# One transformer block on one core: gate and up weights in quarters, two of their sums made by adding transfers, one block more by seven products

## The chip, the core and the metric

The kernel runs on one core of a Trainium2 chip. A core has a matrix engine (TensorE, in the profile PE, with weight loads as PEld), a vector engine (VectorE, DVE), a scalar engine (ScalarE, ACT), GpSimd (POOL) and SyncE (SP). SP and POOL here issue the transfers between the chip's main memory and SBUF, the memory on the core; TensorE writes its products to banks of PSUM, which VectorE and ScalarE read. Each engine works through a fixed list of instructions in order and waits at semaphores. The metric is the device time of one execution in microseconds.

## What is computed

One layer of a hybrid encoder block on 512 tokens of width 1024: a token mixer with two kinds of attention, cross-attention into 256 memory tokens, and a gated FFN with an inner width of 2816. Each has a norm before and after it, and its result is added to the stream. All inputs and outputs are float32. What the change touches is the FFN's first half:

```python
D_MODEL = 1024
D_FF = -(-8 * D_MODEL // 768) * 256          # 2816

def swiglu(h, w_gate_up, w_down):
    g, u = jnp.split(h @ w_gate_up, 2, axis=-1)
    return (jax.nn.silu(g) * u) @ w_down

    h = rms_norm(x, g_ffn_pre[l])
    x = x + rms_norm(swiglu(h, w_gate_up[l], w_down[l]), g_ffn_post[l])
```

## The kernel before

**Numbers in two pieces.** Every float32 factor is split into a rounded piece (`hi`, made by a ScalarE cast to fp32r) and the rest (`lo`, a VectorE subtraction). A product is then three matmuls, hi by hi, hi by lo and lo by hi (`mm3`, lines 139 to 142). Activations are split once and stay in SBUF. Weights are loaded in float32, split, and used.

**The FFN's first half.** The 5632 columns of gate and up weights are worked in 22 blocks of 256 columns, gate and up in turn: block n has columns `(n % 2) * FF + (n // 2) * 256` on. A block is a product of 1024 x 256 weights with the normalised activations, 1024 x 512. Cut into two by two quarters on both sides (four k-blocks of 128 rows by 128 columns for the weights, four k-blocks by 256 tokens for the activations `b11`, `b21`, `b12`, `b22`), it is eight products of 4 x 3 matmuls each (`eight`), 96 matmuls of 128 rows by 256 columns. In `seven` the same result comes from seven such products, 84 matmuls, by Winograd's form of Strassen's method: some products take sums of weight quarters (s1 to s4) and sums of activation quarters (t1 to t4, made once), and VectorE adds the products up. Blocks 0 and 1 are loaded and worked ahead (`load_unit`, `first_ffn`); 2, 3 and 11 are done by `eight`, the other 17 by `seven`.

**Weights on their way.** For a block by seven, `seven_weights` makes four items for a ring in SBUF (`ring_hi`, `ring_lo`): the quarter a11; the sums s2 and s4; the upper row of quarters; and the sums s3 and s1. `load_raw` brings the block by two SP transfers of 512 KB, `lower` and `upper`, in three rotating raw buffers (tag `raw`), with runs of 256 floats in main memory. VectorE makes the four sums (lines 929 to 932) into one of the two halves of the tile `sums`, chosen by the block's parity. Each item is then split into the ring by a ScalarE cast and a VectorE subtraction (lines 902 and 903). A ring slot is filled again once the products that read it are done; single slots for a11 number two, double slots three. `take` emits the fills in the program as slots become free; the framework then puts each engine's instructions in order by priority and inserts the semaphores.

**Products and banks.** `seven` (line 1116) uses four banks. The first product goes to p17's left half, the second to p26's right half, the third to p35's left half, the fourth to p26's left half; then VectorE reads all of p26 (line 1128) and the left half of p35 (line 1129). Products five and six follow, with lines 1134 and 1135 reading them. The seventh goes to p35's right half (line 1137) and is read at line 1138. A product that writes a bank waits until its earlier content has been read. Gate blocks use banks with tags a and o and end in a Silu on ScalarE, up blocks use s and t and end in two multiplications (lines 1148 and 1150).

The tile `sums` takes the place of `y`, the cross-attention's output, in SBUF (tag `sB`). After the 22 blocks comes the product with `w_down`, whose weights use the same ring. POOL has no work in the stretch of the blocks.

Of the kernel before, what the change touches and what calls it, by code (L numbers as in the profile page):

```python
# [36 lines left out]
def hybrid_block_kernel(  # L37
# [33 lines left out]
    def f32(ap):  # L71
        return ap.bitcast(F32)
# [23 lines left out]
    def later(n):  # L96
        tc.cur_priority += n
        try:
            yield
        finally:  # L100
            tc.cur_priority -= n

    units = []
    loaded = []

    def load_unit(w, k0, nkb, c0, ncol, dst=None, skip=0):
        u = len(loaded)
        if dst is None:
            def place(name):
                flat = wp.tile([P, KB * 256 + 48], F32R, tag=name, name=f"{name}{u}", bufs=2)  # L110
                return flat[:, skip : skip + nkb * ncol].rearrange("p (k n) -> p k n", k=nkb)

            hi, lo = place("hi"), place("lo")
        else:
            hi, lo = dst()
        step = nkb if nkb * ncol <= 1024 else 4 if ncol < 512 else 2
        j = 0
        for n in [min(step, nkb - k) for k in range(0, nkb, step)]:
            raw = wp.tile([P, n, ncol], F32, tag="raw", name=f"raw{u}_{j}", bufs=3)
            r0 = (k0 + j) * P  # L120
            nc.sync.dma_start(
                raw,
                w[r0 : r0 + n * P, c0 : c0 + ncol].rearrange("(k p) n -> p k n", p=P),
            )
            act.copy(hi[:, j : j + n, :], raw)  # L125
            dve.tensor_tensor(out=lo[:, j : j + n, :], in0=raw, in1=f32(hi[:, j : j + n, :]), op=ALU.subtract)  # L126
            j += n
        loaded.append((hi, lo))
# [98 lines left out]
    with tc.tile_pool(name="mix", bufs=1, reuse_waits="tile") as bp:  # L227
# [75 lines left out]
        raws = {0: load_v(0, 1)}  # L303
# [77 lines left out]
        for b in range(3):  # L381
            l = bp.tile([P, 2, SEQ], F32R, tag=f"L{b}", name=f"L{b}")
# [206 lines left out]
        order = [(0, g) for g in fox_order] + [(1, 0), (1, 1)]  # L589
        for n, (side, g) in enumerate(order):  # L590
            with later(-20):
                q, kt, kl, v = group_proj(f"{side}{g}")
            if n == 3:
# [4 lines left out]
                for k in range(0, KB, 2):  # L598
                    b = msq[:, 2 * (k > 0) : 2 * (k > 0) + 2, :]
# [44 lines left out]
    with tc.tile_pool(name="cross", bufs=1, reuse_waits="tile") as cp:  # L644
# [249 lines left out]
        def item(at, size, fill):  # L894
            items.append((at, at + size, fill))

        def fill_from(at, shape, src, order=None):
            def fill():
                h, l = split(at, None, shape)
                h2, l2 = (a.rearrange(order) for a in (h, l)) if order else (h, l)  # L900
                v = src()
                act.copy(h2, v)  # L902
                dve.tensor_tensor(out=l2, in0=v, in1=f32(h2), op=ALU.subtract)  # L903
                return h, l

            return fill
# [7 lines left out]
        def double():  # L914
            nslot[1] += 1
            return AS_WEIGHTS + 1024 + 1024 * (nslot[1] % 3)

        def seven_weights(n, c0):
            raw, total = {}, sums[:, n % 2]
            s2, s4, s3, s1 = (total[:, i] for i in range(4))  # L920

            def a11():
                raw["lower"] = load_raw(w_gate_up, 0, 4, c0, 256)
                raw["upper"] = load_raw(w_gate_up, 4, 4, c0, 256)
                return raw["lower"][:, :, :P]

            def s2_s4():
                lower, upper = raw["lower"], raw["upper"]
                dve.tensor_tensor(out=s1, in0=lower[:, :, P:], in1=upper[:, :, P:], op=ALU.add)
                dve.tensor_tensor(out=s2, in0=s1, in1=lower[:, :, :P], op=ALU.add)  # L930
                dve.tensor_tensor(out=s4, in0=s2, in1=upper[:, :, :P], op=ALU.add)
                dve.tensor_tensor(out=s3, in0=lower[:, :, :P], in1=lower[:, :, P:], op=ALU.add)
# [5 lines left out]
            item(at := double(), 1024, fill_from(at, two, lambda: raw["upper"], "p c k n -> p k c n"))  # L938
            item(at := double(), 1024, fill_from(at, two, lambda: total[:, 2:4]))

        def eight_weights(n, c0):
            for k0 in (0, 4):
                item(
                    at := double(), 1024,
                    fill_from(at, dict(k=4, n=256), lambda k0=k0: load_raw(w_gate_up, k0, 4, c0, 256)),
                )

        EIGHT = (2, 3, 11)
        for n in range(2, FB):
            (eight_weights if n in EIGHT else seven_weights)(n, (n % 2) * FF + (n // 2) * 256)  # L950

# [100 lines left out]
        for pair in range(2):  # L1052
            ns = slice(pair * 256, (pair + 1) * 256)
            for b in range(2):
                cs = slice(b * P, (b + 1) * P)
                for acc, (wh_, wl_) in zip(accs[b], first_ffn):
                    for k in range(KB):
                        mm3(
                            acc[:, ns], wh_[:, k, cs], wl_[:, k, cs],
                            bt[pair][:, k // 4, 0, k % 4, :], bt[pair][:, k // 4, 1, k % 4, :], k == 0, k == KB - 1,  # L1060
                        )
# [17 lines left out]
        def eight(tags, done):  # L1079
            accs = [bank(tag) for tag in tags]  # L1080
            for half, bs in enumerate(((b11, b12), (b21, b22))):
                ((h, l),) = take()
                for m in range(2):
                    w = [a[:, :, m * P : (m + 1) * P] for a in (h, l)]
# [28 lines left out]
        def twice(a):  # L1113
            return bass.AP(a.tensor, a.offset, [list(a.ap[0]), [0, 2], list(a.ap[-1])])

        def seven(O, tags, done):

            p17, p26, p35, p4 = (bank(tag) for tag in tags)
            v = cp.tile([P, 256], F32, tag="v", name="v", bufs=2)
            (a11,) = take()  # L1120
            product(p17[:, left], a11, b11)
            act.copy(v, p17[:, left])
            ((h, l),) = take()
            product(p26[:, right], (h[:, 0], l[:, 0]), t2)
# [3 lines left out]
            dve.tensor_tensor(out=O[:, 0], in0=halves(p26), in1=twice(v), op=ALU.add)  # L1128
            dve.tensor_tensor(out=O[:, 1, 0], in0=p35[:, left], in1=O[:, 0, 1], op=ALU.add)
# [8 lines left out]
            dve.tensor_tensor(out=O[:, 1], in0=twice(p35[:, right]), in1=O[:, 1], op=ALU.add)  # L1138
            done(1, 0)
            done(1, 1)  # L1140

# [225 lines left out]
```

## Time and profile before

| | |
|---|---|
| runs | 789.24, 1262.61, 787.30 us; median 789.24 |
| the profiled execution, its own time | 786.43 us |
| its span in the profile | 784.0 us |
| granted TensorE clock, mean | 0.998 of full speed |
| read from main memory | 77.13 MB |
| stretch of the blocks by seven, first to last | 482.57 to 660.52 us |

The run of 1262.61 us is disturbed and is not used. The span runs from the program's first instruction to its last; the execution's own time, 786.43 us, has 2.4 us around it.

How to read it: an engine's busy time counts its instructions from start to end, with overlaps counted once. A matmul's row begins when it starts to stream and ends when its last result is out, so rows of matmuls that follow closely overlap, and the pace of TensorE is read from the distance of starts. A group's row gives line, engine, operation, the tile written and the tiles read, shapes, how often, busy time, mean ns of one, and the idle time just before with what ended it. Transfers are shown with the line and queue that issued them and the time from issue to landing.

### The profile page before, as it was taken

The numbers are of one execution on the slowest core, as the hardware profiler recorded it, in microseconds if no ns is written. First come the engines' busy times: TensorE is split into PE (matmuls) and PEld (weight loads), VectorE is DVE, ScalarE is ACT, GpSimd is POOL, SyncE is SP. The second block draws the span as 40 slices with busy tenths as digits, with TensorE's granted clock in tenths as the row PEclk, the third lists the DMA queues.
The fourth block names the chain that finished last, engine by engine and source line by source line (L and its number), as shares of the span: only waits on it lengthen the run. The fifth ranks groups of instructions, "written<-read, shape, count | busy, mean of one in ns | idle before, by whom it ended". The sixth has DMA issues, their size and how long they took to land.

```text
span 784.0 us, 12758 instructions
## 1 busy us (share of the span) xinstructions
PE 762.2 (97%) x4958; PEld 678.8 (87%) x4958; DVE 592.9 (76%) x1073; ACT 425.4 (54%) x774; POOL 71.1 (9%) x110
## 2 busy tenths in 40 slices
PE   8999999999999999999999999999999999999996
PEld 8887788888778888877778899999999999898985
DVE  6567889879887588545663779998899989986626
ACT  7358888757875348444553635554444446543411
POOL 6001231110321101000001100000000000000001
PEclk9999999999999999999999999999999999999999
DMA  7341112412322725421350202332433332241302
GB/s 245 82 133 55 54 55 68 136 67 80 109 68 92 275 105 164 132 77 58 109 174 14 81 28 82 107 109 81 135 109 108 108 110 105 84 161 55 137 25 108
DMA packets 60747, 80.04 MB, mean 102 GB/s; under 512 B 2704, under 2 KB 43664, under 8 KB 60688
## 3 DMA queue, kind: packets, MB, share of 16 engines
q1 hardware_dynamic: 59264, 74.49, 29.2%
q0 software_dynamic: 1280, 4.72, 1.7%
q8 instruction: 39, 0.64, 0.3%
q14 instruction: 20, 0.16, 0.1%
q10 hardware_dynamic: 144, 0.02, 0.0%
HBM read 77.13 MB, written 2.10 MB: 101 GB/s over the span
## 4 chain that ended last, share of the span: by engine, by line
PE 72%; DVE 11%; ACT 7%; issue 4%; DMA 3%; POOL 2%; SPq 0%; DVEq 0%; POOLq 0%; ACTq 0%
PE ps_a L141 14%; PE ps_a L140 14%; PE ps_a L142 14%; PE ps_s L142 4%; PE ps_s L140 4%; PE ps_s L141 4%; DVE ring_lo L903 3%; PE ps_t L534 2%; PE ps_t L140 2%; PE ps_t L141 2%; PE ps_t L142 2%; DMA raw<-in_dram 2%; PE ps_o L543 2%; PE ps_s L515 1%; PE ps_o L140 1%
## 5 line engine op out<-in xcount | busy, mean ns | idle before, releaser
L902 ACT CAST ring_hi<-fraw 128x1024 fp32r<-128x1024 f32 (+1 forms) x62 | 57.5, 932 | 64.3 <-PE ps_t L142 17.6
L126 DVE TENSOR_TENSOR lo<-raw,hi 128x1024 fp32r<-128x1024 f32 x56 | 68.2, 1224 | 22.3 <-ACT hi L125 22.0
L903 DVE TENSOR_TENSOR ring_lo<-fraw,ring_hi 128x1024 fp32r<-128x1024 f32 (+1 forms) x62 | 66.5, 1076 | 21.4 <-ACT ring_hi L902 21.0
L142 PE MATMUL ps_a<-hTh,lo 128*128 128x512 f32 x192 | 76.8, 400 | 0.6 <-DVE lo L126 0.6
L141 PE MATMUL ps_a<-hTl,hi 128*128 128x512 f32 x192 | 76.1, 396 | 0.0
L140 PE MATMUL ps_a<-hTh,hi 128*128 128x512 f32 x192 | 75.9, 395 | 0.1
L125 ACT CAST hi<-raw 128x1024 fp32r<-128x1024 f32 x56 | 57.8, 1048 | 23.9 <-PE ps_a L141 15.0
L902 ACT CAST ring_hi<-sums 128x1024 fp32r<-128x1024 f32 x34 | 35.7, 1050 | 54.9 <-PE ps_a L141 24.2
L903 DVE TENSOR_TENSOR ring_lo<-sums,ring_hi 128x1024 fp32r<-128x1024 f32 x34 | 41.6, 1223 | 4.3 <-ACT ring_hi L902 4.1
L142 PEld LDWEIGHTS ps_a<-hTh,lo 128*128 128x128 f32 x192 | 36.1, 188 | 7.3 <-DVE lo L126 1.0
L141 PEld LDWEIGHTS ps_a<-hTl,hi 128*128 128x128 f32 x192 | 36.1, 188 | 6.3
L140 PEld LDWEIGHTS ps_a<-hTh,hi 128*128 128x128 f32 x192 | 36.2, 188 | 6.1 <-ACT hi L125 0.3
L529 ACT ACTIVATE p<-p,nm 128x128 f32<-128x128 f32 (+1 forms) x64 | 36.2, 565 | 8.4 <-DVE nm L519 7.6
L140 PE MATMUL ps_a<-b,ring_hi 128*128 128x256 f32 x140 | 38.8, 277 | 0.0
L141 PE MATMUL ps_a<-b,ring_hi 128*128 128x256 f32 x140 | 38.8, 277 | 0.0
L142 PE MATMUL ps_a<-b,ring_lo 128*128 128x256 f32 x140 | 38.8, 277 | 0.0
L140 PE MATMUL ps_s<-b,ring_hi 128*128 128x256 f32 x128 | 35.5, 277 | 0.0
L141 PE MATMUL ps_s<-b,ring_hi 128*128 128x256 f32 x128 | 35.5, 277 | 0.0
L142 PE MATMUL ps_s<-b,ring_lo 128*128 128x256 f32 x128 | 35.5, 277 | 0.0
L536 ACT CAST pth<-ps_t 128x128 fp32r<-128x128 f32 (+1 forms) x64 | 27.0, 424 | 14.5 <-PE ps_t L534 13.8
L537 DVE TENSOR_TENSOR ptl<-ps_t,pth 128x128 fp32r<-128x128 f32 (+1 forms) x64 | 30.7, 487 | 5.0 <-ACT pth L536 3.7
L534 PE MATMUL ps_t<-ident,p 128*128 128x128 f32 x160 | 28.1, 275 | 1.1 <-DVE p L531 0.8
(534 smaller groups left out, 2619.8 us busy)
## 6 DMA issues: line engine op xcount, KB each, us to landing
raw<-in_dram SPq DMA_DIRECT2D x64, 512.0 KB, 3.6
fraw<-in_dram SPq DMA_DIRECT2D x62, 512.0 KB, 3.5
cb<-in_dram SPq DMA_DIRECT2D x8, 256.0 KB, 2.6
xo<-in_dram POOLq DMA_DIRECT2D x4, 512.0 KB, 5.5
out_dram<-yd SPq DMA_DIRECT2D x8, 256.0 KB, 2.0
rawv<-in_dram SPq DMA_DIRECT2D x3, 520.0 KB, 6.2
xt<-in_dram SPq DMA_DIRECT2D x3, 512.0 KB, 6.9
gb<-in_dram POOLq DMA_DIRECT2D x3, 512.0 KB, 4.8
```

The costliest lines, as they stand in the source:

```text
L125: act.copy(hi[:, j : j + n, :], raw)
L126: dve.tensor_tensor(out=lo[:, j : j + n, :], in0=raw, in1=f32(hi[:, j : j + n, :]), op=ALU.subtract)
L140: pe.matmul(dst, sh, mh, start=first, stop=False)
L141: pe.matmul(dst, sh, ml, start=False, stop=False)
L142: pe.matmul(dst, sl, mh, start=False, stop=last)
L529: act.activation(p[:, :n], p[:, :n], AF.Exp, bias=nm, scale=-1.0, accum_out=sm)
L534: pe.transpose(tp[:, k * P : (k + 1) * P], p[:, k * P : (k + 1) * P], ident)
L536: act.copy(span(ph, i), t3)
L537: dve.tensor_tensor(out=span(pl, i), in0=t3, in1=f32(span(ph, i)), op=ALU.subtract)
L543: pe.matmul(acc[:, a:], v[:, k, vh, :], m[:, k * PTS + a : k * PTS + SEQ], start=k == 0 and m is ph, stop=k == NT - 1 and m is pl,)
L902: act.copy(h2, v)
L903: dve.tensor_tensor(out=l2, in0=v, in1=f32(h2), op=ALU.subtract)
```

## The change

On the host, `w_gate_up` is laid out anew before the launch, so that each quarter of a block (128 partitions by 4 x 128 floats) lies in contiguous rows of 2 KB. Quarter (r, m) of the block is k-blocks 4r to 4r + 3 and columns 128m to 128m + 127. All reads of gate and up weights go through the new function `quarters`.

In `seven_weights` the four sums become two: s2 and s4 stay on VectorE. s1 and s3 are made by transfers: SP loads quarter (0, 1) into each, then POOL issues a transfer that adds quarter (1, 1) to s1 and quarter (0, 0) to s3. a11 has a load of its own (256 KB), and the lower k-blocks' other half is read twice, once for each sum; the row of quarters with r = 1 is one load of 512 KB (`raw["upper"]`). Items are split in the order in which they are loaded, without the reordering of before.

Block 11 is done by `seven` instead of `eight`. In `seven`, the last product goes to p26's left half instead of p35's right half. The functions that work by eight products read their weights in the new order.

```diff
+    def quarters(c, r, m=None):
+        row = (c // 256 * 2 + r) * 2 * P
+        if m is None:
+            return w_gate_up[row : row + 2 * P, :].rearrange("(m p) n -> p m n", p=P)
+        return w_gate_up[row + m * P : row + (m + 1) * P, :]
...
+            if w is w_gate_up:
+                nc.sync.dma_start(raw.rearrange("p k n -> p (k n)").rearrange("p (m n) -> p m n", m=2), quarters(c0, j // 4))
+            else:
+                nc.sync.dma_start(
...
+        def load_half(c0, r):
+            raws[0] += 1
+            raw = wp.tile([P, 2, 4 * P], F32, tag="raw", name=f"fraw{raws[0]}", bufs=3)
+            nc.sync.dma_start(raw, quarters(c0, r))
+            return raw.rearrange("p c (k n) -> p c k n", k=4)
...
             def a11():
-                raw["lower"] = load_raw(w_gate_up, 0, 4, c0, 256)
-                raw["upper"] = load_raw(w_gate_up, 4, 4, c0, 256)
-                return raw["lower"][:, :, :P]
+                raws[0] += 1
+                raw["a11"] = wp.tile([P, 4, P], F32, tag="raw", name=f"fraw{raws[0]}", bufs=3)
+                nc.sync.dma_start(flat(raw["a11"]), quarters(c0, 0, 0))
+                for s, (r, m) in ((s1, (1, 1)), (s3, (0, 0))):
+                    nc.sync.dma_start(flat(s), quarters(c0, 0, 1))
+                    nc.gpsimd.dma_start(flat(s), quarters(c0, r, m), accum_op=ALU.add)
+                raw["upper"] = load_half(c0, 1)
+                return raw["a11"]
 
             def s2_s4():
-                lower, upper = raw["lower"], raw["upper"]
-                dve.tensor_tensor(out=s1, in0=lower[:, :, P:], in1=upper[:, :, P:], op=ALU.add)
-                dve.tensor_tensor(out=s2, in0=s1, in1=lower[:, :, :P], op=ALU.add)
-                dve.tensor_tensor(out=s4, in0=s2, in1=upper[:, :, :P], op=ALU.add)
-                dve.tensor_tensor(out=s3, in0=lower[:, :, :P], in1=lower[:, :, P:], op=ALU.add)
+                dve.tensor_tensor(out=s2, in0=s1, in1=raw["a11"], op=ALU.add)
+                dve.tensor_tensor(out=s4, in0=s2, in1=raw["upper"][:, 0], op=ALU.add)
                 return total[:, 0:2]
...
-        EIGHT = (2, 3, 11)
+        EIGHT = (2, 3)
...
-            product(p35[:, right], (h[:, 1], l[:, 1]), t1)
-            dve.tensor_tensor(out=O[:, 1], in0=twice(p35[:, right]), in1=O[:, 1], op=ALU.add)
+            product(p26[:, left], (h[:, 1], l[:, 1]), t1)
+            dve.tensor_tensor(out=O[:, 1], in0=twice(p26[:, left]), in1=O[:, 1], op=ALU.add)
...
+    at = len(arrs) - len(_WEIGHTS) + _WEIGHTS.index("w_gate_up")
+    arrs[at] = arrs[at].reshape(2, 4, P, -1, 2, P).transpose(3, 0, 4, 2, 1, 5).reshape(-1, 4 * P)
```

More of the change, by code (lines that the diff above doesn't have):

```diff
@@ L120, in load_unit @@
             r0 = (k0 + j) * P
[L121 to L124, printed above, removed]
+            if w is w_gate_up:
+                nc.sync.dma_start(raw.rearrange("p k n -> p (k n)").rearrange("p (m n) -> p m n", m=2), quarters(c0, j // 4))
+            else:
+                nc.sync.dma_start(
+                    raw,
+                    w[r0 : r0 + n * P, c0 : c0 + ncol].rearrange("(k p) n -> p k n", p=P),
+                )
             act.copy(hi[:, j : j + n, :], raw)
@@ L895, in item, with fill_from @@
             items.append((at, at + size, fill))
-        def fill_from(at, shape, src, order=None):
+        def fill_from(at, shape, src):
             def fill():
                 h, l = split(at, None, shape)
-                h2, l2 = (a.rearrange(order) for a in (h, l)) if order else (h, l)
                 v = src()
-                act.copy(h2, v)
-                dve.tensor_tensor(out=l2, in0=v, in1=f32(h2), op=ALU.subtract)
+                act.copy(h, v)
+                dve.tensor_tensor(out=l, in0=v, in1=f32(h), op=ALU.subtract)
                 return h, l
@@ L916, in double, with flat @@
             return AS_WEIGHTS + 1024 + 1024 * (nslot[1] % 3)
+        def flat(a):
+            return a.rearrange("p k n -> p (k n)")
+        def load_half(c0, r):
[3 more added lines that the diff above has]
+            return raw.rearrange("p c (k n) -> p c k n", k=4)
         def seven_weights(n, c0):
@@ L937, in seven_weights @@
             item(at := double(), 1024, fill_from(at, two, s2_s4))
-            item(at := double(), 1024, fill_from(at, two, lambda: raw["upper"], "p c k n -> p k c n"))
+            item(at := double(), 1024, fill_from(at, two, lambda: raw["upper"]))
             item(at := double(), 1024, fill_from(at, two, lambda: total[:, 2:4]))
         def eight_weights(n, c0):
[L942 to L946, printed above, removed]
-        EIGHT = (2, 3, 11)
+            for r in range(2):
+                item(at := double(), 1024, fill_from(at, dict(c=2, k=4, n=P), lambda r=r: load_half(c0, r)))
+        EIGHT = (2, 3)
         for n in range(2, FB):
@@ L1083, in eight @@
                 for m in range(2):
-                    w = [a[:, :, m * P : (m + 1) * P] for a in (h, l)]
+                    w = [a[:, m] for a in (h, l)]
                     for n, ns in enumerate((left, right)):
```

9 lines of the change are left out of this document (6 added, 3 removed).

## The prediction

> **What bounds the kernel now.** I read the page first, then a table of time windows over the stage that the change touches, then single instructions of TensorE (PE) and VectorE (DVE) in it. The page gives the span and each engine's load.
>
> ```profile
> span 784.0 us, 12758 instructions
> PE 762.2 (97%) x4958; PEld 678.8 (87%) x4958; DVE 592.9 (76%) x1073; ACT 425.4 (54%) x774; POOL 71.1 (9%) x110
> PE 72%; DVE 11%; ACT 7%; issue 4%; DMA 3%; POOL 2%; SPq 0%; DVEq 0%; POOLq 0%; ACTq 0%
> ```
>
> TensorE is busy for 97% of the span and is 72% of the chain that ended last, so the time is TensorE's work plus its waits. The change touches the gate and up products of the FFN. In the windows below, the first row holds the whole run of blocks from the first one done by seven products to the last; the others are single blocks. The columns are stretch, its length, and for each engine busy time (instructions), then the granted clock, DMA share and GB/s. Instructions that overlap a border are counted on both sides, so counts run two or three high.
>
> ```profile
> 482.57:660.52 177.95, 176.19 (x1526) 174.69 (x1525) 165.23 (x238) 87.29 (x132) 0.00 (x0) 1.00 0.33 104
> 482.57:492.77 10.20, 9.80 (x86) 9.61 (x85) 9.63 (x14) 5.20 (x7) 0.00 (x0) 1.00 0.32 103
> 551.92:562.80 10.88, 10.88 (x99) 10.88 (x97) 9.28 (x14) 3.77 (x6) 0.00 (x0) 1.00 0.49 150
> 562.80:572.32 9.52, 9.52 (x87) 9.52 (x85) 8.77 (x12) 4.36 (x6) 0.00 (x0) 1.00 0.35 109
> 611.92:621.70 9.78, 9.78 (x86) 9.78 (x85) 9.30 (x14) 4.87 (x8) 0.00 (x0) 1.00 0.34 109
> ```
>
> 551.92:562.80 is block 11, the one block of this stretch still done by eight products; 562.80:572.32 is block 12, by seven, with no wait in it. The stretch holds 17 blocks of seven and one of eight. Free of waits they would take 17 x 9.52 + 10.88 = 172.72 us; they took 177.95. So 5.23 us are lost here. One loss looks like this (start, length, engine, line, matmul, and the idle time before it with what ended it):
>
> ```profile
> 490.50 0.28 PE L141 MATMUL ps_a<-tlo,ring_hi 128*128 128x256 f32 x1
> 490.62 0.28 PE L142 MATMUL ps_a<-tlo,ring_lo 128*128 128x256 f32 x1
> 491.29 0.39 PE L140 MATMUL ps_a<-thi,ring_hi 128*128 128x256 f32 x1 [0.40 <-DVE G L1129]
> ```
>
> Starts go from 0.12 us apart to 0.67: the seventh product, which writes the right half of bank p35, waits until VectorE has read that bank's left half (line 1129). VectorE was late because a sum of weights stood between:
>
> ```profile
> 489.62 0.69 DVE L1128 TENSOR_TENSOR G<-ps_a,v 128x512 f32<-128x512 f32 x1
> 490.22 0.68 DVE L931 TENSOR_TENSOR sums<-sums,fraw 128x512 f32<-128x512 f32 x1
> 490.82 0.42 DVE L1129 TENSOR_TENSOR G<-ps_a,G 128x256 f32<-128x256 f32 x1
> ```
>
> VectorE is busy for 165.23 of 177.95 us (93%), a second engine nearly full. Such waits sum, by the list of waits in the FFN, to:
>
> ```profile
> PE ps_a L140 <- DVE G L1129: 1.5, 5, 0.4
> PE ps_t L140 <- DVE U L1129: 0.3, 1, 0.3
> ```
>
> These 1.8 us are much less than the 5.23 from counting. A matmul's row lasts 0.28 us where starts are 0.12 us apart, so a busy row covers part of each wait; and after some waits the pace is lower: block 17 (611.92:621.70) took 9.78 us without any idle time. I take the count. The Trainium skill (Perfetto Trace Analysis, section Identifying the Most-Contended Engine) says that matmul busy time misjudges TensorE because matmuls are pipelined, and to use the share of weight loads; the trace agrees with its first half. By weight loads the loss would be 177.95 - 174.69 = 3.26 us and the time about 2 us above mine.
>
> **The change part by part.** (1) Block 11 by seven products. TensorE does 87 instead of 99 matmuls by these windows: 10.88 - 9.52 = 1.36 us saved, all on the path.
>
> (2) The seventh product goes to p26's left half instead of p35's right half. It then waits for line 1128, the reader of p26, instead of line 1129. In the case above line 1128 ended at 489.62 + 0.69 = 490.31 and TensorE was ready after its matmul of 490.62: no wait. The edit alone removes this wait. What is late next is line 1128 itself, with about 0.4 us to spare here.
>
> (3) VectorE's load. For removed and added work, these rows (busy time, mean ns):
>
> ```profile
> L929 DVE TENSOR_TENSOR sums<-fraw,fraw 128x512 f32<-128x512 f32 x17 | 11.7, 687 | 1.1 <-DMA fraw<-in_dram 1.1
> L932 DVE TENSOR_TENSOR sums<-fraw 128x512 f32<-128x512 f32 x17 | 11.7, 689 | 2.3 <-DMA fraw<-in_dram 2.0
> L903 DVE TENSOR_TENSOR ring_lo<-sums,ring_hi 128x1024 fp32r<-128x1024 f32 x34 | 41.6, 1223 | 4.3 <-ACT ring_hi L902 4.1
> L1128 DVE TENSOR_TENSOR U<-ps_s,v 128x512 f32<-128x512 f32 x8 | 5.5, 685 | 0.0
> L1129 DVE TENSOR_TENSOR U<-ps_t,U 128x256 f32<-128x256 f32 x8 | 3.4, 424 | 0.2
> L1138 DVE TENSOR_TENSOR U<-ps_t,U 128x512 f32<-128x512 f32 x7 | 4.8, 692 | 0.7
> ```
>
> Two sums leave each of the 17 blocks: 11.7 + 11.7 = 23.4 us. Block 11 adds two sums (1.4), one and a half more splits (1.8) and five reads of banks, two as wide as 0.69 and three of 0.42 (2.6): 5.8 us. VectorE goes from 165.2 to about 147.6 us of 171: 86%. None of it is on the path by itself; it is the cover for (2).
>
> (4) The two sums become transfers. Each seven-block now has SP loads of 256 KB for a11, 256 KB twice for the sums' first term, 512 KB for the lower row of quarters, and two POOL transfers of 256 KB that add. Before it was two SP loads of 512 KB. SP issues four instead of two, and POOL, idle in this stretch (0.00 above), 36 in all.
>
> ```profile
> fraw<-in_dram SPq DMA_DIRECT2D x62, 512.0 KB, 3.5
> cb<-in_dram SPq DMA_DIRECT2D x8, 256.0 KB, 2.6
> xo<-in_dram POOLq DMA_DIRECT2D x4, 512.0 KB, 5.5
> gb<-in_dram POOLq DMA_DIRECT2D x3, 512.0 KB, 4.8
> 258.71 2.16 POOL L683 DMA_DIRECT2D xo<-in_dram  x4
> ```
>
> The last figure of the first four rows is microseconds from issue to landing; the fifth row is POOL's own issuing time, 2.16 / 4 = 0.54 us each. No row shows an adding transfer. Nearest rows: a POOL load of 512 KB, 4.8 to 5.5 us; an adding one of 256 KB moves as much if it reads its target too, so I take 5.5 us. The ends I keep are 2.6 us (a plain 256 KB load on SP) and 11 us (twice the slower POOL load). The chain of one sum is serial: SP load 2.6 to 3.5, then POOL 5.5, so 8.1 to 9.0 us. Is it hidden? The load may start when the same half of the sums buffer, used two blocks earlier, has been split; block 18 shows the times:
>
> ```profile
> 602.84 1.23 DVE L903 TENSOR_TENSOR ring_lo<-sums,ring_hi 128x1024 fp32r<-128x1024 f32 x1
> 616.33 0.69 DVE L930 TENSOR_TENSOR sums<-sums,fraw 128x512 f32<-128x512 f32 x1
> 623.11 0.28 PE L140 MATMUL ps_a<-thi,ring_hi 128*128 128x256 f32 x1
> ```
>
> The buffer is free at 604.07; the first sum that stays on VectorE (line 930) began at 616.33, which leaves 12.3 us against 9.0. TensorE needs the result only at 623.11; two sums and a split later than 616.33 would be about 619, so some 4 us more pass before it stalls. An adding transfer of 5.5 us, and even one of 8.8 (12.3 - 3.5), costs nothing; one of about 13 us begins to cost. If that cover is gone, every microsecond more is paid once in two blocks, about nine times. Bytes per block grow from 1.0 to 1.75 MB, or 2.25 with the targets read again: the DMA share goes from 0.33 to between 0.58 and 0.74. The transfers do not fill the queues.
>
> What is queued behind the new waits: on POOL only the next adding transfer. On SP the sums' loads wait for the split at 604.07, and behind them stands the lower row's load, which waits for its own buffer until the sum of the block before (line 930) anyway, later than that. On VectorE, line 930 now waits for POOL, and behind it stand the reads of the banks (lines 1128 to 1138) that release TensorE: that is how lateness would reach the path. The quarters' layout makes rows of 2 KB and more contiguous and drops the reordering in one split: taken at nothing, since those loads hide behind VectorE's buffers.
>
> The sum: 786.43 (the profiled run) - 1.36 - 5.23 = 779.84 us if all waits and the slower pace after them go. The profiled run is the lowest of those shown; the undisturbed others are 787.30 and 789.24, and the three average 787.66, 1.2 above it. I add that: 781.0 us.
>
> **The rivals.** *A: the block alone counts.* Waits return at line 1128, or the slower pace stays though the waits go. Against the first: 0.4 us to spare and less work on VectorE. For the second: block 17 ran 0.26 us slow with no wait, and 18 such blocks would lose 4.7 us. Time: 781.0 + 4.7 = 785.7. *A2: POOL and VectorE share a path to SBUF.* The SBUF page of the Trainium skill (SBUF — State Buffer, section Who interferes with whom) says that a VectorE instruction with two SBUF inputs contends with POOL's reads, and that VectorE in its two-port modes blocks POOL's building of transfers. Were VectorE stopped during each issue, 36 x 0.54 = 19.4 us would eat the 17.6 us gained in (3); the swap in (2) would still hold, and the time is between 781 and 786. Against it, VectorE beside those four issues ran two splits at the usual length, and POOL's issues were not drawn out:
>
> ```profile
> 259.15 2.36 DVE L126 TENSOR_TENSOR lo<-raw,hi 128x1024 fp32r<-128x1024 f32 x2 [0.25 <-ACT hi L125]
> ```
>
> *B: the start pays.* The first sums reuse the buffer of y, the normalised output of the cross-attention, and the first adding transfers meet VectorE's densest stretch; a wait of 5 to 10 us there, with bank reads behind it, gives 786 to 791. For it: VectorE's order is fixed beforehand. *C, on the other side: the adding transfer is slow.* At 16 us, three beyond the point of 13, nine pairs pay 3 us each: 781 + 27 = 808 us. It decides above 13 us, and each further one adds nine. For it: no trace shows such a transfer, and it reads and writes SBUF. Against it: 13 is 2.4 times the slowest POOL load of twice the bytes.
>
> **How the numbers follow.** Forecast (779 to 784): 0.60. A (784 to 787): 0.12. A2 (781 to 786, counted apart from the forecast): 0.05. B (786 to 795): 0.13. C: 0.09, nearly all over 2% slower. Something unknown of over 2% faster: 0.01. Two per cent is 15.7 us, about what a measurement of this kernel can tell from no change; the largest gain that I can count is 6.6, so faster is 0.01, slower 0.09, same 0.90. The range runs from 778.5 (all of it and no allowance, with run scatter) to 790, which takes in A, A2 and about half of B and leaves out about 0.17. The likeliest case's own range is 779 to 784.
>
> **What would show it.** Block 11's window at 9.52 us with 87 matmuls: part 1. No wait of the seventh product: part 2. Lines 929 and 932 gone and VectorE near 86%: part 3. POOL transfers landing within 9 us and VectorE never idle before line 930: part 4. I am wrong if VectorE or ACT idles for POOL's transfers and TensorE behind them, or if blocks still take over 9.6 us.

## The result, and the profile after

| | before | after |
|---|---|---|
| median of the runs, same chip | 789.24 us | 823.91 us (821.27 to 826.25) |
| profiled execution: own time, span | 786.43, 784.0 us | 821.27, 819.5 us |
| granted TensorE clock, mean | 0.998 | 0.986 |

Slow or disturbed runs (1262.61 us before; 793.13 us in e3 and 1073.21 us in e6, both below) are left out of the medians. The ratio is 1.044, 95% interval 1.041 to 1.047: over 4% slower, where no measurable change was forecast. The head of the page after:

```profile
span 819.5 us, 12901 instructions
PE 775.4 (95%) x4946; PEld 689.1 (84%) x4946; DVE 575.0 (70%) x1048; ACT 426.8 (52%) x777; POOL 102.8 (13%) x146
```

VectorE lost 18 us of work, as meant, and TensorE's busy time grew though it has 12 matmuls fewer. Where the time went is told by one window in each trace, from the first matmul that uses a sum of activations in block 4, the first block by seven, to the start of the product with `w_down` (columns: stretch, length, then busy time and instructions of PE, PEld, DVE, ACT, POOL, then granted clock, DMA share, GB/s). Before:

```profile
483.93:660.52 176.59, 174.83 (x1514) 173.32 (x1513) 164.40 (x237) 86.07 (x131) 0.00 (x0) 1.00 0.32 104
```

After:

```profile
484.00:696.27 212.27, 187.60 (x1502) 183.11 (x1501) 150.77 (x218) 87.92 (x134) 27.66 (x32) 0.95 0.61 148
```

The stretch begins at the same time and is 35.7 us longer; what follows it takes as long as before (784.0 - 660.5 and 819.5 - 696.3, 123 us each). So the whole loss, 35.5 us of span, lies in the blocks by seven, about 2 us in each. VectorE is busy for 71% of the stretch, and DMA is at 0.61. The list of waits after, from 430 to 720 us (who waits and for whom; us in total, times, longest us):

```profile
DVE sums L952 <- DMA sums<-in_dram: 50.3, 17, 4.3
...
PE ps_a L150 <- DVE G L1149: 14.8, 7, 3.6
PE ps_s L150 <- DVE U L1149: 8.5, 6, 2.7
```

Line 952 is the former line 930, the sum s2, which reads s1; in nearly every block VectorE now stands still for its adding transfer. Line 1149 is the former 1128. These are the engines behind which the prediction said lateness would come to the path; what it had excluded is that the transfer is late. It is not a slow transfer (KB each, median us from issue to landing):

```profile
sums<-in_dram SPq DMA_DIRECT2D x36, 256.0 KB, 2.8
sums<-in_dram POOLq DMA_DIRECT2D x36, 256.0 KB, 5.1
```

One turn of a block shows what it waits for. The timeline after, rows chosen (start, length, engine, line, operation, idle time before it and its releaser):

```profile
616.99 1.22 DVE L912 TENSOR_TENSOR ring_lo<-sums,ring_hi 128x1024 fp32r<-128x1024 f32 x1
618.23 0.80 SPq L946 DMA_DIRECT2D sums<-in_dram  x2
622.06 1.72 POOL L947 DMA_DIRECT2D sums<-in_dram  x2 [10.26 <-DVE ring_lo L912]
626.38 0.69 DVE L952 TENSOR_TENSOR sums<-sums,fraw 128x512 f32<-128x512 f32 x1 [3.56 <-DMA sums<-in_dram]
626.99 1.22 DVE L912 TENSOR_TENSOR ring_lo<-fraw,ring_hi 128x1024 fp32r<-128x1024 f32 x1
...
629.58 0.69 DVE L1159 TENSOR_TENSOR U<-ps_s,U 128x512 f32<-128x512 f32 x1
630.18 1.22 DVE L912 TENSOR_TENSOR ring_lo<-sums,ring_hi 128x1024 fp32r<-128x1024 f32 x1
631.43 0.33 SPq L946 DMA_DIRECT2D sums<-in_dram  x1
```

Read it as a circle. The split of a fourth item (616.99) frees one half of `sums`; SP loads the first term there (618.23); when that has landed, POOL adds (622.06); s2 starts (626.38); 5.0 us of VectorE's list later the next fourth split ends (631.40), and SP issues again (631.43): 13.2 us for one block. The mean of fifteen such turns is 12.2 us (s2 at 493.94 and at 676.84 us, first and last):

```profile
493.94 0.69 DVE L952 TENSOR_TENSOR sums<-sums,fraw 128x512 f32<-128x512 f32 x1 [3.28 <-DMA sums<-in_dram]
676.84 0.69 DVE L952 TENSOR_TENSOR sums<-sums,fraw 128x512 f32<-128x512 f32 x1 [3.88 <-DMA sums<-in_dram]
```

TensorE would need 9.52. In the kernel before, VectorE's list had another order at this place. Between the rows of 602.84 and 616.33 us that the prediction shows stands the fourth split of the block between:

```profile
606.99 0.69 DVE L930 TENSOR_TENSOR sums<-sums,fraw 128x512 f32<-128x512 f32 x1
...
613.14 1.23 DVE L903 TENSOR_TENSOR ring_lo<-sums,ring_hi 128x1024 fp32r<-128x1024 f32 x1
```

There the order was: split of a block m (602.84), s2 of m+1 (606.99), split of m+1 (613.14), s2 of m+2 (616.33), which uses the half freed at 602.84. So s2 of block n stood behind the fourth split of block n-1. After, with the split of m at 616.99, s2 of m+2 (626.38) stands ahead of the split of m+1 (630.18). The two halves of `sums` are still there, but the list lets only one be under way: a split can't run before the s2 of the other half, and that waits for the transfers which the split before it released.

### The profile page after: what moved, and what is told of

Read it like the earlier page. It is cut to its first block, busy times and chain, and to the rows that moved or that the text cites. A ratio compares the mean times of both kernels' runs of the same rounds, so it can differ in the third digit from the quotient of the medians.

```text
span 819.5 us, 12901 instructions
## 1 busy us (share of the span) xinstructions
PE 775.4 (95%) x4946; PEld 689.1 (84%) x4946; DVE 575.0 (70%) x1048; ACT 426.8 (52%) x777; POOL 102.8 (13%) x146
## 5 line engine op out<-in xcount | busy, mean ns | idle before, releaser
L911 ACT CAST ring_hi<-sums 128x1024 fp32r<-128x1024 f32 x36 | 37.7, 1046 | 39.9 <-PE ps_a L151 11.9
L947 POOL DMA_DIRECT2D sums<-in_dram x36 | 31.2, 981 | 198.4 <-DVE ring_lo L912 104.7
L912 DVE TENSOR_TENSOR ring_lo<-sums,ring_hi 128x1024 fp32r<-128x1024 f32 x36 | 43.9, 1219 | 9.6 <-ACT ring_hi L911 9.6
L952 DVE TENSOR_TENSOR sums<-sums,fraw 128x512 f32<-128x512 f32 x18 | 12.5, 693 | 53.9 <-DMA sums<-in_dram 50.3
L150 PE MATMUL ps_a<-thi,ring_hi 128*128 128x256 f32 x72 | 23.0, 319 | 14.8 <-DVE G L1149 14.8
L1164 ACT ACTIVATE G<-G 128x256 f32<-128x256 f32 x36 | 14.0, 413 | 38.9 <-DVE G L1156 23.6
```

The costliest lines, as they stand in the source:

```text
L150: pe.matmul(dst, sh, mh, start=first, stop=False)
L911: act.copy(h, v)
L912: dve.tensor_tensor(out=l, in0=v, in1=f32(h), op=ALU.subtract)
L947: nc.gpsimd.dma_start(flat(s), quarters(c0, r, m), accum_op=ALU.add)
L1164: act.activation(G[:, n, m], G[:, n, m], AF.Silu, scale=(1.0, -1.0)[m])
```

## The experiments

**Theory:** this loop, made by where s2 and s4 stand in VectorE's list. **Rivals:** the adding transfers cost time by themselves (their length, their number, their share of SBUF or DMA); the swap of banks or block 11 does; VectorE's load does; ScalarE's waits for loads of a11 do, 36.9 us in the trace after. Each comparison has the kernel before on the same chip (medians 789.66 us for e1 to e4, 788.34 for e5 to e8, 788.86 for e9 to e11). A profile's stretch is measured between the same two events as above.

| kernel | median, us | ratio, 95% interval | stretch in its profile, us |
|---|---|---|---|
| e1 swap alone | 788.70 | 0.9972 to 1.0017 | 175.5 |
| e2 order | 788.03 | 0.9965 to 1.0003 | 179.2 |
| e3 three places | 786.03 | 0.9935 to 0.9986 | 173.5 |
| e4 s3 alone adds | 788.09 | 0.9966 to 1.0000 | 176.2 |
| e5 s1 alone adds | 823.66 | 1.0434 to 1.0465 | 213.1 |
| e6 POOL loads, adds nothing | 804.74 | 1.0190 to 1.0232 | 196.6 |
| e7 no adding transfers | 790.07 | 0.9994 to 1.0025 | 181.6 |
| e8 order and three places | 792.00 | 1.0028 to 1.0058 | 183.4 |
| e9 e3 again | 787.47 | 0.9957 to 1.0010 | 178.0 |
| e10 e9 with p35 | 793.88 | 1.0040 to 1.0088 | 179.3 |
| e11 e9 with block 11 by eight | 790.39 | 0.9979 to 1.0026 | 181.1 |

**e1: of the change, the swap of banks alone**, in the kernel before.

```diff
-            product(p35[:, right], (h[:, 1], l[:, 1]), t1)
-            dve.tensor_tensor(out=O[:, 1], in0=twice(p35[:, right]), in1=O[:, 1], op=ALU.add)
+            product(p26[:, left], (h[:, 1], l[:, 1]), t1)
+            dve.tensor_tensor(out=O[:, 1], in0=twice(p26[:, left]), in1=O[:, 1], op=ALU.add)
```

> The kernel before with one edit of the change: the seventh product goes to p26's left half instead of p35's right half. No quarters, no adding transfers, block 11 still by eight. If the prediction's step on this wait is right, the seventh product waits for line 1128 instead of 1129, the 5.2 us of waits and slower pace in the stretch of the blocks go, and the time is about 4 to 5 us under the kernel before (784 to 786 us against 789). Rival: the wait only moves to line 1128 and the time stays within 1 us.

The same time as before, as the rival has it: not the source of the loss, and by itself no gain that can be measured. TensorE's waits from 483 to 668 us, in its trace:

```profile
PE ps_a L140 <- DVE G L1128: 0.7, 1, 0.7
PE ps_s L140 <- DVE U L1128: 0.3, 1, 0.3
```

Six waits for line 1129 became two for line 1128, 1.8 us became 1.0.

**e2: the changed kernel with s2 and s4 put back in VectorE's list**, behind the fourth split of the block before. `issue_after` only sets an order within VectorE's list. That is the only edit, but not the only difference: by the traces the lists of TensorE and POOL are the same to the instruction as after, SP's differs in one load, and other instructions of VectorE and ScalarE moved along with s2 and s4.

```diff
-                dve.tensor_tensor(out=s2, in0=s1, in1=raw["a11"], op=ALU.add)
-                dve.tensor_tensor(out=s4, in0=s2, in1=raw["upper"][:, 0], op=ALU.add)
+                with tc.issue_after(fourth[n - 1]) if n - 1 in fourth else nullcontext():
+                    dve.tensor_tensor(out=s2, in0=s1, in1=raw["a11"], op=ALU.add)
+                    dve.tensor_tensor(out=s4, in0=s2, in1=raw["upper"][:, 0], op=ALU.add)
```

> The changed kernel, with VectorE's sums s2 and s4 of block n put behind the split of block n-1's fourth item in VectorE's list; nothing else differs. Theory (order loop): s2 of a block waits for its adding transfer while the split that lets the next adding transfer start stands behind it, so each block costs one whole chain split - load - add - sum, 12.2 us instead of 9.5. With the new order the chain has two blocks' time, the waits on the adding transfers fall from 50 us to under 5, and the time falls from 824 to 780 to 790 us. Rival (slow transfers): adding transfers are late because they, or the fuller DMA queues, are slow; then the order does not help and the time stays above 815. Rival (raw buffers): ScalarE's 37 us of waits for loads of a11, which start only when the sum before has freed a buffer, set the pace; then the time stays above 805, with these waits left.

35.9 us come back by putting two instructions of 0.69 us elsewhere in each block. The transfers are as many and nearly as long (4.9 us in the median against 5.1), and VectorE's waits for them fall from 50.3 to 2.4 us. In its timeline the split that frees a half and the s2 that uses it now lie 11 us apart:

```profile
617.00 1.22 DVE L914 TENSOR_TENSOR ring_lo<-sums,ring_hi 128x1024 fp32r<-128x1024 f32 x1
618.13 0.69 DVE L957 TENSOR_TENSOR sums<-sums,fraw 128x512 f32<-128x512 f32 x1
618.25 0.80 SPq L950 DMA_DIRECT2D sums<-in_dram  x2
621.52 0.88 POOL L951 DMA_DIRECT2D sums<-in_dram  x1 [7.88 <-DMA sums<-in_dram]
629.20 0.68 DVE L957 TENSOR_TENSOR sums<-sums,fraw 128x512 f32<-128x512 f32 x1
```

The s2 at 618.13 belongs to the other half; the one that needs the load of 618.25 is that of 629.20, and VectorE does not idle before it.

**e3: another way out**: s2 still stands ahead of the fourth split of the block before, as after (some other instructions of VectorE and ScalarE moved). s1 and s3 get three rotating places instead of two; s2 and s4, which one block uses at a time, share one.

```diff
-        sums = big.tile([P, 2, 4, 4, P], F32, tag="sB", name="sums")
+        sums = big.tile([P, 8, 4, P], F32, tag="sB", name="sums")
...
-            raw, total = {}, sums[:, n % 2]
-            s2, s4, s3, s1 = (total[:, i] for i in range(4))
+            at = 2 + n % 3 * 2
+            raw, total = {}, (sums[:, 0:2], sums[:, at : at + 2])
+            s2, s4, s3, s1 = (t[:, i] for t in total for i in range(2))
```

> The changed kernel, with s1 and s3 in three rotating places instead of two and s2 and s4 in one instead of two (the tile keeps its size). VectorE's list still has the sum of block n before the fourth split of block n-1. Theory (order loop): the load of s1 for block n+3 now waits for the split of block n, so the loop spans two blocks (about 8 us of transfers and 4 us of VectorE in 19 us); the waits go and the time is 780 to 790 us. Rival (slow transfers): above 815. Rival (raw buffers): above 805.

The loss goes here too: a load may now start one block earlier. Its transfers even take longer than those of the slow kernel, and fill more of the queues (0.69 against 0.61):

```profile
sums<-in_dram SPq DMA_DIRECT2D x36, 256.0 KB, 4.6
sums<-in_dram POOLq DMA_DIRECT2D x36, 256.0 KB, 6.0
```

and its window over the stretch:

```profile
484.12:657.57 173.45, 171.10 (x1502) 170.32 (x1501) 153.03 (x220) 88.66 (x135) 25.96 (x30) 1.00 0.69 177
```

The rival of the a11 loads falls with it: e9, which is e3 once more, has 36.8 us of these waits in its trace, as many as after, without the loss.

**e4 and e5: half the adding transfers.** e4 keeps s3's and gives s1 back to VectorE; e5 keeps s1's and gives s3 back; in both the lower k-blocks come as one load of 512 KB. Both have 18 adding transfers and three sums on VectorE. s1 is read by s2 in the middle of the block, s3 only by the fourth split at its end.

```diff
-                for s, (r, m) in ((s1, (1, 1)), (s3, (0, 0))):
+                for s, (r, m) in ((s3, (0, 0)),):
...
+                dve.tensor_tensor(out=s1, in0=raw["lower"][:, 1], in1=raw["upper"][:, 1], op=ALU.add)
```

> The changed kernel, with only s3 made by an adding transfer; s1 is summed on VectorE from two loads of 512 KB. VectorE keeps three sums of a block. s3 is used only by the fourth split, so nothing waits for it early. Theory (order loop): no sum on VectorE waits for POOL, and the time is 780 to 788 us. Rival (slow transfers): half of the transfers and of their cost stay, about 805 us.

> Of the changed kernel only the sum s1 is made by an adding transfer; s3 is again a VectorE instruction (L952... of this kernel, read late in the block). So it has 18 adding transfers, as many as the kernel that kept only s3, and like that one three sums a block on VectorE. Theory (a loop in VectorE's order): s2 of block n, which waits for this transfer, still stands ahead of the split of the fourth item of block n-1, and that split still releases the half of the sums buffer into which the next transfer's load goes. The loop split, load, adding transfer, s2, split is intact, so a block still takes 11.5 to 12.5 us and the time is 805 to 824 us, over 2% slower than before. Rival (the number of adding transfers or their share of SBUF or DMA costs the time): the same as the kernel with s3 alone, 786 to 790 us.

Both came out as the loop has it: 788.09 us (0.09 above the range) and 823.66 us, with the same number of transfers. e5 has half the transfers of the changed kernel and all of its loss. What counts is not how many transfers there are but that one of them lies in the circle.

**e6: how long the transfer in the circle may be.** POOL's transfers load without adding.

```diff
-                    nc.gpsimd.dma_start(flat(s), quarters(c0, r, m), accum_op=ALU.add)
+                    nc.gpsimd.dma_start(flat(s), quarters(c0, r, m))
```

> The changed kernel with the POOL transfers loading without adding: the same 36 transfers, issues, waits and VectorE order; left out is the first term of s1 and s3, which the second one overwrites. Theory (one chain of split, SP load, POOL transfer, sum and split per block): the time falls by 17 to 18 times what the transfer is shorter. If a plain POOL transfer of 256 KB takes 2.6 to 4.5 us instead of 5.1, blocks take 9.7 to 11.7 us and the time is 790 to 815 us, still slower than before. Rival (what costs is the adding: its reads of SBUF and the like beside VectorE and ScalarE): the loss goes wholly and the time is 782 to 788 us. If the adding costs nothing against a plain transfer on POOL, the time stays at 820 to 825 us and the loop is set by the two transfers in a row alone.

Half the loss stays. This is the cleanest of the comparisons: in its trace the lists of all engines are the same as after, to the instruction, and only the transfer is shorter; what it computes is of no use, since the first terms are left out. Two traces give the price of adding. Of each pair of lines the first has POOL's own issuing time in ns and the second the time from issue to landing in us, shortest, median and longest. Without adding (e6):

```profile
L947 POOL DMA_DIRECT2D sums<-in_dram x36: 536/536/586, 454.0 to 659.3; - x36
...
DMA to landing us min/median/max: 2.8/2.9/4.5
```

and the same for the adding transfers of e5, each alone in its block:

```profile
L946 POOL DMA_DIRECT2D sums<-in_dram x18: 835/845/930, 455.1 to 673.0; - x18
...
DMA to landing us min/median/max: 3.9/4.1/4.8
```

The one in the circle is 1.2 us shorter without adding (the 5.1 above is a median over both transfers of a block; the second has the first ahead of it). Fifteen turns of the circle, 12.2 us each after, now take 11.3:

```profile
492.28 0.69 DVE L952 TENSOR_TENSOR sums<-sums,fraw 128x512 f32<-128x512 f32 x1 [0.76 <-DMA sums<-in_dram]
661.69 0.69 DVE L952 TENSOR_TENSOR sums<-sums,fraw 128x512 f32<-128x512 f32 x1 [2.33 <-DMA sums<-in_dram]
```

By the ratios the time fell by (1.044 - 1.0211) x 788.34 = 18.1 us, 1.06 us for each of 17 turns: nearly microsecond for microsecond, as a circle must. The expectation's range and slope hold, but with 1.2 us as the difference; from its 5.1 us the slope would have given 37 us.

**e7: the quarters' layout, block 11 and the swap, with all four sums on VectorE** and loads of 512 KB.

> The changed kernel without the adding transfers: quarters layout, block 11 by seven products and the seventh product in p26 stay, all four sums of weights are VectorE's, from two loads of 512 KB as before. What the prediction took the transfers to be good for is the VectorE time that they free: without them VectorE has about 171 us of work in a stretch of 171 us. If that relief is worth something, the stretch takes 176 to 182 us and the time is 787 to 795 us, 2 to 8 us above the kernel with the sums in three places (786.5 by its runs, 782.6 in its profile). Rival (VectorE's load never cost TensorE anything but the order did): 783 to 787 us, the same as there. Either way no wait of 4 us on a transfer, and not 2% slower than before: the layout and block 11 are not where the 35 us went.

790.07 us, within the expected range: layout, block 11 and swap neither cost nor bring anything measurable when VectorE is left full, 168.97 of 181.56 us in its window:

```profile
484.61:666.17 181.56, 176.66 (x1502) 175.61 (x1501) 168.97 (x247) 88.33 (x134) 0.00 (x0) 0.99 0.32 100
```

e3 and e9, which free VectorE, are 2.6 to 4.0 us below it by medians. They were timed on other chips, so this is an indication only.

**e8: both repairs at once.**

> The changed kernel with both repairs: s1 and s3 in three rotating places, s2 and s4 in a place of their own, and s2 and s4 of block n placed behind the fourth split of block n-1 in VectorE's order. Theory: either repair alone opens the loop, so together they give no more than the one with three places: 781 to 788 us, a ratio of 0.993 to 1.000, with no wait of VectorE on the adding transfers. If something else of the transfers still costs time beside the loop, it is under 4 us here. Rival (each repair brings back a part only): below 780 us.

Both sides missed: 792.0 us, a little slower than before. The transfers are in time (3.3 us of waits for them). TensorE waits for the bank reads behind s2 and s4 (line 1155 here is line 1149 after), and ScalarE's casts wait for s4:

```profile
ACT ring_hi L913 <- DVE sums L959: 25.2, 15, 3.4
PE ps_s L150 <- DVE U L1155: 6.5, 6, 2.7
```

The trace of e2 has nearly the same waits, so the forced place alone does not tell why e8 is the slower of the two:

```profile
ACT ring_hi L913 <- DVE sums L958: 26.9, 15, 3.5
PE ps_s L150 <- DVE U L1154: 4.6, 6, 1.4
```

What differs most among TensorE's waits is the single one of 2.7 us; why it comes, and why e8 is slower, stays open.

**e9, e10, e11: the terms of the sum, each by itself**, in the version with three places.

> The version with s1 and s3 in three rotating places once more, on the chip of the two that follow, so that they can be compared with it. It was 786.5 us by its runs and 782.6 us in its profile. Expected 782 to 788 us, a ratio of 0.993 to 1.000 to the kernel before.

> The version with three places, but the seventh product goes to the right half of p35 again, as in the kernel before; VectorE's order stays the same to the instruction. It prices part 2 of the prediction by itself. If the swap is worth something once VectorE has air, TensorE waits for the second reading of a bank (L1151, which stands behind a sum of weights) in most blocks, some 0.3 to 0.6 us each, and the time is 2 to 9 us above the version with three places. Rival (VectorE's relief alone takes the waits away, the swap is worth nothing): within 2 us of it.

> The version with three places, but block 11 is done by eight products again. It prices part 1: by the matmuls that block 11 saves, 12 of 0.113 us, the time is 1.4 us above the version with three places, and block 11 takes 10.9 instead of 9.5 us in its trace. If taking the block out of the row of blocks by seven disturbs or calms its neighbours, the difference is up to 3 us either way.

e9 came out as expected, at 787.47 us. With the seventh product back in p35 the time is 6.4 us higher (793.88 - 787.47; the intervals of the two ratios do not touch). The time is in the expected range, the cause is not shown: e10's profile, the fastest of its executions, has three waits at line 1151, not one in most blocks, and longer ones than expected:

```profile
PE ps_a L150 <- DVE G L1151: 3.4, 3, 2.3
```

The stretch of that profile is only 1.3 us longer than e9's (179.3 and 178.0). So the 6.4 us may be such waits in the slower executions, or the slower of the two paces told of at the end.

With block 11 by eight it is 2.9 us higher by medians and 1.6 by the ratios (1.0003 - 0.9983, times 788.9); their intervals overlap, so 1.4 us fits and no difference does too. In its trace block 11 takes 10.88 us as before:

```profile
556.25:567.13 10.88, 10.88 (x98) 10.88 (x97) 8.06 (x11) 3.66 (x6) 0.00 (x0) 1.00 0.59 150
```

## Why the prediction was wrong, point by point

**The step that failed** is in part (4): "The buffer is free at 604.07; the first sum that stays on VectorE (line 930) began at 616.33, which leaves 12.3 us against 9.0." Both times are right for the kernel before. The error is to take the distance over. It is not a property of the buffer but of VectorE's list, and that list is made anew when instructions are added and removed. In the new list s2 stands one fourth split earlier, and the room is that of one block less the 5.0 us of VectorE's list in the turn above: at TensorE's 9.52 us a block, 9.52 - 5.0 = 4.5 us for load and adding transfer together, where that turn shows 8.1 (618.23 to 626.38). So the point "of about 13 us" for the adding transfer was in truth at about 4.5 - 2.8 = 1.7 us behind a load of 2.8; even e6's plain transfer of 2.9 us failed it. The price was wrong with it: not "once in two blocks, about nine times", but in every turn, as e6 shows. The sign that the prediction named for this came: VectorE idled 50.3 us before the former line 930. e2 shows that the order decides it: with s2 behind the split again, about the old room (10.9 us there) and the old time are back.

Two sentences of the prediction lean on the same assumption. "For it: VectorE's order is fixed beforehand" was said for rival B; the order is fixed for one program, but not the same for two. And the passage "What is queued behind the new waits" went through POOL, SP and VectorE for what comes after line 930 and found the bank reads, but not the next fourth split, the one that releases the next load. The step that was missing is to follow the wait round, from the instruction that waits to the one that frees its buffer, and to ask whether the second stands behind the first.

**Part (1), block 11: right.** In e3 the block's window is the predicted one, 9.52 us with 87 matmuls; in the changed kernel the loop covers it. In the runs the gain is too small to tell from none (e11).

```profile
552.86:562.38 9.52, 9.52 (x87) 9.52 (x86) 7.67 (x12) 4.93 (x8) 1.76 (x3) 1.00 0.80 196
```

**Part (2), the swap: the wait went, the time did not come.** "The edit alone removes this wait" holds for the waits for line 1129, but smaller ones for line 1128 came, the slower pace stayed, as rival A had it, and e1 won nothing. With VectorE relieved the swap is worth 6.4 us (e10). That this is near the 5.23 of the sum is luck: the 5.23 were to be won against the kernel before, and e10, which has all but the swap, is itself slower than that kernel (1.0064).

**Part (3), VectorE's load: right.** 153.03 of 173.45 us in e3, 88%, against 86% forecast. But the gains did not come to 6.6 us in the end, once the loop was opened: e3 and e9 are 3.6 and 1.4 us below the kernel before by medians. Part of the rest shows in the first block of the stretch, where rival B had put it; in e3 it took 11.75 us, with 1.7 us in which TensorE was idle:

```profile
482.75:494.50 11.75, 10.06 (x86) 9.67 (x85) 11.68 (x16) 6.23 (x9) 1.11 (x2) 1.00 0.39 112
```

In e9 another part is the slower pace, below.

**Part (4), the transfer's length: right, and not the question.** 5.1 us against 5.5.

**Rival A2 falls.** In e3's trace, where VectorE works on while POOL issues, s2 and s4 took 684 and 685 ns in the mean, as before (687 and 689), and a sum and a split beside two adding issues took their usual length:

```profile
569.85 1.74 POOL L948 DMA_DIRECT2D sums<-in_dram  x2 [7.17 <-DMA sums<-in_dram]
570.34 0.69 DVE L954 TENSOR_TENSOR sums<-sums,fraw 128x512 f32<-128x512 f32 x1
570.94 1.22 DVE L912 TENSOR_TENSOR ring_lo<-fraw,ring_hi 128x1024 fp32r<-128x1024 f32 x1
```

The contention between VectorE instructions with two SBUF inputs and POOL's reads that the Trainium skill (SBUF — State Buffer, section Who interferes with whom) states showed no price beside these issues.

**Rival C** had the right sign for a wrong reason: lateness at line 930 paid block by block is what came, but with a transfer of 5 us and in every block, not above 13 and in every second.

**Still open:** why the framework placed s2 there. The trace shows the place and e2 its price; no run tried what decides it. The best version here, three places, is 0.2 to 0.4% below the kernel before, with 1 inside one of its two intervals.

## What to carry to other kernels

A gap measured between two instructions of one engine is only as good as their order, and an edit that adds a transfer or takes instructions out can change that order; before counting on such a gap, compare the two lists, or keep the order by hand. When a transfer takes over work that an engine did in place, look for the circle: if the instruction that waits for the transfer stands ahead of the one that frees the buffer for the next, double buffering is lost and, where the turn is longer than a block's work, every microsecond of the transfer is paid in each turn. Two remedies worked here, one more buffer or the consumer moved behind the release; the two together were 0.6 to 0.8% slower by the ratios.

## What the runs showed of the hardware

**The price of adding on the way in.** A POOL transfer of 256 KB took 2.9 us from issue to landing (e6), and 4.1 when it adds, with one in a block (e5); POOL itself was held for 0.54 and 0.84 us. The 4.1 is no constant: in e4, also with one in a block, the median was 5.5. By the Trainium skill (DMA: Bandwidth & Descriptors, section Anatomy of one DMA — SWDGE (gpsimd) path), about 2.0 us and the bytes over 436 GB/s, the plain one would take 2.6 us (an estimate); e6 agrees within 0.3. For adding that section gives no figure.

**The clock drops in the waits.** After TensorE's longest waits in the changed kernel its matmuls follow at half their pace for some 3 us. The timeline there, and windows of one microsecond:

```profile
515.76 0.52 PE L150 MATMUL ps_a<-thi,ring_hi 128*128 128x256 f32 x1 [3.60 <-DVE G L1149]
```

```profile
516.00:517.00 1.00, 1.00 (x6) 1.00 (x6) 1.00 (x2) 0.16 (x1) 0.00 (x0) 0.50 1.01 139
...
520.00:521.00 1.00, 1.00 (x12) 1.00 (x11) 1.00 (x1) 0.52 (x2) 0.00 (x0) 1.00 0.77 252
```

TensorE was idle for 3.60 us, then runs at 0.50 with 6 matmuls in a window instead of 12, and is at full clock again by 520. The Trainium skill (TensorE: Matmul & The Clock Gate, section What's actually happening) states half the clock after an idle window of about 3.4 us, until TensorE has been busy as long. The trace agrees with the length: its clock records have six spells at half clock in the stretch, each of 3.41 us. It does not agree with the condition, if one wait is meant: this is the only spell after a wait that long, and the other five stand at waits of 1.8 to 2.7 us. After a wait of 2.41 us, before the matmul at 598.77 us, the clock stayed full; after this one of 1.81 us it dropped:

```profile
610.38 0.39 PE L150 MATMUL ps_a<-thi,ring_hi 128*128 128x256 f32 x1 [1.81 <-DVE G L1149]
```

```profile
611.42:614.83 3.41, 3.41 (x19) 3.41 (x18) 0.85 (x2) 1.04 (x1) 0.38 (x1) 0.50 0.90 124
```

This is most of why TensorE's busy time rose: 212.27 us at 0.95 are some 10.6 us of clock. By the turns above it seems to cost little on top, since the circle of transfers sets the block's length whether TensorE waits or runs slowly; that was not tried by itself.

**Two paces.** A block by seven without a wait takes 9.52 us or 9.89, to the hundredth. e3 and e9 are the same program; in e3's profile twelve blocks in a row took 114.23 us, 9.52 each:

```profile
533.82:648.05 114.23, 114.23 (x1010) 114.23 (x1009) 99.20 (x144) 55.37 (x83) 18.28 (x22) 1.00 0.72 183
```

and in e9's eight in a row took 79.14 us, 9.89 each, at the same granted clock of 1.00:

```profile
535.95:615.09 79.14, 79.14 (x674) 79.14 (x673) 66.75 (x98) 36.90 (x56) 13.86 (x16) 1.00 0.74 188
```

That is 118 ns from start to start instead of 113, over 84 matmuls. 17 such blocks are 6.3 us, about half of the range between executions (782.4 to 793.9 us in e9) and nearly the prediction's whole gain of 6.6; that it makes this scatter is not shown. The pace mostly changes at a wait and stays, but in e9 it also changed at 523.86 us between matmuls 124 ns apart, without one; what chooses it was not found.
